# A two-layer gMLP and latent-attention trunk: the rotary score product with a 128-row stationary operand, its key zero-padded by halves

## The chip, the cores and the metric

One core of one Trainium2 chip runs the whole program in a single launch. The metric is the device time of one execution in microseconds; three runs of the kernel before gave 1175.08, 1179.63 and 1184.22 us, with a median of 1179.63 us. One more execution was recorded by the profiler, and every time of a single instruction comes from that one.

## The reference

Batch 1, 256 tokens, width 2048. A gMLP layer is followed by a layer of multi-head latent attention with 16 heads; every sub-layer is modulated by a shift, a scale and a gate worked out from a conditioning vector. What the change touches is the score of the attention: each head's key and query have a part of 128 dimensions without position and a rotary part of 64, and the rotary key is one and the same for all heads.

```python
k_rope = apply_rope(rms_norm(k_r, g_kr), cos, sin)          # (B, S, 64): one for all heads
...
s = (jnp.einsum('bqhd,bkhd->bhqk', qn_b, k_nope)            # 128 dimensions, per head
     + jnp.einsum('bqhr,bkr->bhqk', qr_b, k_rope)).astype(jnp.float32) * scale
s = jnp.where(k_pos[None, :] <= q_pos[:, None], s, -jnp.inf)
p = jax.nn.softmax(s, axis=-1).astype(v.dtype)
return jnp.einsum('bhqk,bkhd->bqhd', p, v)
```

The queries come in two blocks of 128. The rotary key of a token, k_rope, is normalised and rotated once, before the keys of the heads are made.

## The kernel before, in words

**The products over weights.** Every large product reads its weights from memory in pieces of 1 MB (`raw`, L304; four buffers, shared with the modulation's pieces `araw`, L178). ScalarE rounds a piece to `hi` (L160), VectorE subtracts to get `lo` (L162), and TensorE adds three products (hi by hi, hi by lo, lo by hi, L324) into PSUM banks. There are four pairs of `hi` and `lo` buffers, so ScalarE writes a new `hi` when TensorE is done with an old one. The output projection (`b_w_out`, 16 pieces) is the last of these products, and its results are gated, added to the residual and stored (L598, L599, L884).

**The modulation.** A step of `Ada` (L175) loads 1 MB of a modulation weight and multiplies it with the conditioning row on VectorE (L187). The last sixteen steps make the gate `ga1`; they are spread over the attention and the output projection, and TensorE turns four of their columns at a time into a piece of the gate (L229).

**The attention.** `keys(i)` and `queries(i)` make two heads at a time. A query product ends in `pq`; its heads are normalised and rotated, and TensorE turns them over (L816 for the 128 dimensions without position, L817 for the rotary ones). The two rotary parts of a pair, 64 dimensions each, are turned over together: `qrT` has the even head in rows 0 to 63 and the odd head in rows 64 to 127 (L819). `ev_dkv` makes the rotary key: it is written twice side by side into `kd`, turned over in one piece (L735), and copied to `krT` (L736), which thus holds the same 64 rows in both halves of its 128.

When both parts of a pair are there, `attend(h)` is queued for its two heads (L760) and one such entry is issued after each item of the main loop (L351). `attend(h)` issues the scores of head h and the output of the head before.

`scores(h)` has four products, two for each block of queries: L842 with the 128 dimensions without position (stationary operand 128 by 128), L843 with the 64 rotary ones (stationary operand 64 by 128, in rows 0 to 63 for an even head and 64 to 127 for an odd one, by `pb`). The first block has 128 keys, the second 256. The operands are float32, and each such product is two instructions of the same shape on TensorE, with a weight load each. VectorE then scales, masks and takes the maximum (L847), ScalarE takes the exponential (L850).

`output(h)` turns the probabilities over on TensorE (L860), copies them back (L862), multiplies with the values (L863 to L865) and gates (L868). After an odd head, four turns (L877) bring the pair's result into the form that the output projection reads.

The framework orders the instructions of each engine when the program is built, and each engine then issues its own in that order. The DMA queue of SyncE is in the order of the program text.

Of the kernel before, what the change touches and what calls it, by code (L numbers as in the profile page):

```python
# [9 lines left out]
F32 = mybir.dt.float32  # L10
# [4 lines left out]
PSUM = bass.MemoryType.PSUM  # L15

P = 128
D = 2048
S = 256
# [4 lines left out]
DR = 64  # L24
DV = 128
R = 512
EPS = 1e-6
KD = D // P
NB = 1024
# [25 lines left out]


class Banks:
    """The eight PSUM banks: some for accumulation throughout, the others shared out among streams of tiles by phase."""
    def __init__(self, tc):
        self.tc, self.phase, self.ctx = tc, -1, ExitStack()  # L60
        self.mm = self.ctx.enter_context(tc.tile_pool(name="psm", bufs=MM, space=PSUM))
# [25 lines left out]
def trunk_kernel(ctx: ExitStack, tc: tile.TileContext, a: dict, out: bass.AP):  # L87
    nc = tc.nc
    ctx.enter_context(tc.manual_schedule(engines={nc.sync.engine}))
    const = ctx.enter_context(tc.tile_pool(name="const", bufs=1))  # L90
# [5 lines left out]
    banks = Banks(tc)  # L96
# [8 lines left out]
    def bank(name, tag="aux"):  # L105
        return banks.tile(tag, name)

# [1 line left out]
    crow = slot("crow")  # L109
    nc.sync.dma_start(crow[0:1, :], a["c"])  # L110
    xt = []
# [15 lines left out]
    nhalf = const.tile([P, 4], F32, name="nhalf")  # L127
    nc.vector.memset(nhalf, -0.5)

# [1 line left out]
    def rstd_of(ms, n, scale=1.0):  # L131
        """(ms * scale + EPS) ** -0.5"""
        t = sml.tile([P, 4], F32, tag="rs0", name="rs0")
        r = sml.tile([P, 4], F32, tag="rs1", name="rs1")
        nc.vector.tensor_scalar(out=t[:, :n], in0=ms, scalar1=scale, scalar2=EPS, op0=ALU.mult, op1=ALU.add)
        nc.gpsimd.tensor_tensor(out=r[:, :n], in0=t[:, :n], in1=nhalf[:, :n], op=ALU.pow)
        return r[:, :n]
# [3 lines left out]
        nc.scalar.activation(j, src, AF.Square, scale=scale, accum_out=dst)  # L141

    def rms_rstd(pieces):
        """1/rms of the rows made of pieces."""
        n = len(pieces)
        ss = sml.tile([P, 4], F32, tag="ss4", name="ss4")
        for i, p in enumerate(pieces):
            squares(ss[:, i:i + 1], p, "a")
        return rstd_sum(ss, n, sum(p.shape[-1] for p in pieces))
# [12 lines left out]
            nc.vector.tensor_tensor(out=lo, in0=src, in1=hi.bitcast(F32), op=ALU.subtract)  # L162

    def behind(ins):
        """What follows is issued after ins, where there is one, on its engine."""
        return tc.issue_after(ins.ins) if ins else nullcontext()

    hold, queue, chain = [None], [False], []
# [43 lines left out]
            ada[background.pop(0)].step()  # L212

    class Gate:
        """A gate as rows on all partitions, by pieces of 512 columns."""
        def __init__(self, n):
            self.ada, self.rows, self.done = ada[n], None, set()

# [12 lines left out]
            return g  # L231

    class Norm:
        """x / rms(x), transposed."""
        def __init__(self, xt, name):
            self.xt = xt
            self.ts = [slot(f"{name}T{i}") for i in range(2)]
# [11 lines left out]
            nc.scalar.copy(dst, p.rearrange("p (k t) -> p k t", t=P))  # L249

        def rows(self, t):
            """The whole of token tile t, scaled as rows."""
            for q in range(4):
                self.sums(t, q)
            r = rstd_sum(self.st[t], 4, D)
            for q in range(4):
                x = self.xt[t][:, q * 512:(q + 1) * 512]
                nc.vector.tensor_scalar_mul(x, x, r)
                self.flip(t, q)
# [3 lines left out]
            self.flip(t, q)  # L263

        def finish(self, t):
            """1/rms of token tile t, broadcast over the partitions."""
            if self.rb is None:
                self.rb = const.tile([P, S], F32, name=self.name + "rb")
            r = rstd_sum(self.st[t], 4, D)
            p = bank("px")  # L270
            nc.tensor.transpose(p[:, :P], r.broadcast_to([P, P]), ident)
            return p[:, :P]
# [27 lines left out]
            return lambda c, w: self.at(w, 2 * kk + c)  # L300

    def load_split(w, kk, n, nk=2):
        """nk chunks of the contraction of w as exact pairs hi + lo; a pair of tiles holds up to NB columns in all."""
        raw = wraw.tile([P, nk, n], F32, tag="raw", name="raw")  # L304
        nc.sync.dma_start(raw, w[kk * nk * P:(kk + 1) * nk * P, :].rearrange("(c p) n -> p c n", p=P))
        per = max(1, NB // n) if n < NB else 1
        parts = []
        for c0 in range(0, nk, per):
            hi = wsp.tile([P, per, n], F32R, tag="hi", name="hi")
            lo = wsp.tile([P, per, n], F32R, tag="lo", name="lo")  # L310
            split(raw[:, c0:c0 + per, :], hi, lo)
            parts += [(hi[:, c, :], lo[:, c, :]) for c in range(per)]
        return parts

    def mms(ps, t, lh, wt, widths, first, last, apart=False):
        """Adds the chunks wt of the contraction, for token tile t, to the banks ps."""
        offs = [sum(widths[:i]) for i in range(len(widths))]
        for some in ([[i] for i in range(len(widths))] if apart else [range(len(widths))]):
            for c, (hi, lo) in enumerate(wt):
                for which, rhss in ((0, (hi, lo)), (1, (hi,))):  # L320
                    lt = lh(c, which)[:, t * P:(t + 1) * P]
                    for rhs in rhss:
                        for i in some:
                            nc.tensor.matmul(ps[i][:, :widths[i]], lhsT=lt, rhs=rhs[:, offs[i]:offs[i] + widths[i]],  # L324
                                             start=(first and c == 0 and which == 0 and rhs is hi),
                                             stop=(last and c == len(wt) - 1 and which == 1))
# [1 line left out]
    later = deque()  # L328

    def drive(items):  # L330
        """items: (prepare, compute, after). The next item is prepared before the present one is computed, or, where
        the present one ends in a chain that the next waits for, right before what follows it."""
        items = iter(items)
        nxt = next(items, None)
        ready = nxt[0]() if nxt else None
        while nxt:
            cur, got = nxt, ready
            nxt = next(items, None)
            late = len(cur) > 3
            if nxt and not late:  # L340
                queue[0] = True
                ready = nxt[0]()
                queue[0] = False
            cur[1](got)
            if nxt and late:
                queue[0] = True
                ready = nxt[0]()
                queue[0] = False
            cur[2]()
            if later:  # L350
                later.popleft()()  # L351

    class Block:
        """A product over a block of columns of w, cut along the contraction in steps of two chunks."""
        def __init__(self, lhs, w, nkk, widths, evac):
            self.lhs, self.w, self.nkk, self.widths, self.evac = lhs, w, nkk, widths, evac
            self.n = sum(widths)
# [52 lines left out]
                    bg(quota * tail if n < stop else 0.0)  # L410
                yield (prep, comp, post, "late") if then else (prep, comp, post)

# [1 line left out]
    norm0 = Norm(xt, "x")  # L414
    for t in range(NT):
        norm0.rows(t)
# [29 lines left out]
    blocks = [[in_block("v", i, None), vt[i], lambda t, n, ps, i=i: ev_v(i, t, n, ps)] for i in range(4)]  # L446
# [173 lines left out]
            b = Block(lhs_split(lambda kk: yT[kk // 4][:, (kk % 4) * 2:(kk % 4) * 2 + 2, :]), a["a_w_out"][:, i * NB:(i + 1) * NB], GW // P // 2, [512, 512], ev_o)  # L620
            yield from b.items(AQ, tail=TAIL, after=early1 if i else None, then=late1 if i else None, before=fetch, stop=STOP if i else 99)

# [1 line left out]
    at = {}  # L624

    def attention_constants():
# [26 lines left out]
        nc.vector.tensor_tensor(out=dst[:, :, 32:64], in0=dst[:, :, 32:64], in1=m[:, :, 0:32], op=ALU.add)  # L653

    rinv = const.tile([P, NT, 16], F32, name="rinv")
    krT = const.tile([P, S], F32, name="krT")
    lat, szb, yb = {}, {}, {}
    gate1 = Gate("ga1")
    w_b = a["b_w_in"]
# [22 lines left out]
        return lambda c, w: at["h"].at(w, 2 * kk + c)  # L682

    def latent(which, t, pieces, gname):
        """Normalises the row made of pieces (PSUM), and keeps it transposed as hi + lo."""
        r = rms_rstd(pieces)
        cn = scratch([P, R], "cn")
        o = 0
        for p in pieces:
            n = p.shape[-1]  # L690
            nc.scalar.activation(cn[:, o:o + n], p, AF.Identity, scale=r)
            o += n
        p = bank("px", "tr")
        for j in range(4):
            nc.tensor.transpose(p[:, j * P:(j + 1) * P], cn[:, j * P:(j + 1) * P], ident)
        if which not in lat:
            lat[which] = slot("lat" + which, F32R).rearrange("p (w k t) -> p w k t", w=2, t=S)
        lt = lat[which]
        h = scratch([P, 4, P], "hl")
        for j in range(4):  # L700
            nc.vector.tensor_scalar_mul(h[:, j, :], p[:, j * P:(j + 1) * P], col[gname][:, j:j + 1])
        split(h, lt[:, 0, :, t * P:(t + 1) * P], lt[:, 1, :, t * P:(t + 1) * P])
# [18 lines left out]
    def ev_dkv(t, n, ps):  # L721
# [3 lines left out]
        w = R - 288  # L725
# [7 lines left out]
        nc.vector.tensor_copy(kd[:, 1, :], kd[:, 0, :])  # L733
        p = bank("px", "tr")
        nc.tensor.transpose(p[:, :P], kd.rearrange("p a b -> p (a b)"), ident)  # L735
        hold[0] = nc.vector.tensor_copy(krT[:, t * P:(t + 1) * P], p[:, :P])  # L736

    def lhs_lat(which):
        return lambda c, w: lat[which][:, w, c, :]
# [86 lines left out]
    soft = {}  # L826

    def attend(h):
        """The scores of head h, and the output of the head before, whose softmax runs meanwhile."""
        if h < 16:  # L830
            scores(h)
        if h > 0:
            output(h - 1)

    def scores(h):
        i, j = divmod(h, 2)
        kT, qT, qrT = (pairs[i][n] for n in ("kT", "qT", "qrT"))
        pS = bank("pS")
        pb = j * DR
        for t, (c0, c1) in enumerate(TQ):  # L840
            nk = c1 - c0
            nc.tensor.matmul(pS[:, c0:c1], lhsT=qT[:, j, t * P:(t + 1) * P], rhs=kT[:, j, 0:nk], start=True, stop=False)  # L842
            nc.tensor.matmul(pS[:, c0:c1], lhsT=qrT[pb:pb + DR, t * P:(t + 1) * P], rhs=krT[pb:pb + DR, 0:nk], start=False, stop=True)  # L843
        pr = scratch([P, P + S], "pr", "b")
        mx = sml.tile([P, 4], F32, tag="mx", name="mx")
        for t, (c0, c1) in enumerate(TQ):
# [100 lines left out]
```

## Time and profile before

| | |
|---|---|
| runs | 1175.08, 1179.63, 1184.22 us; median 1179.63 |
| span of the profiled execution, first to last instruction | 1176.9 us; its own time outside the span is not recorded |
| mean granted TensorE clock | 0.989 |
| busy, share of the span | TensorE 95%, its weight load 78%, VectorE 82%, ScalarE 53%, GpSimd 7% |
| read from memory | 331.10 MB, 283 GB/s over the span |
| first and last score product | 973.6 and 1099.5 us after the start of the span |
| output projection's products | about 1058 to 1169 us |

A timeline row gives the start in us, the duration in us, the engine (PE is TensorE's products, PEld its weight loads, DVE VectorE, ACT ScalarE, POOL GpSimd), the line of the kernel, the operation, the tile written and those read, the shape, and how many instructions the row covers; in brackets stands the idle time before it and what ended it. Successive products overlap in the records, so what a product costs the stream is the distance from its start to the next start, not its duration. A row "128*128 128x256" is a product with 128 active rows and columns whose moving operand has 256 columns. A row of the table by windows has the window, its length, and for PE, PEld, DVE, ACT and POOL the busy time with the number of instructions, then the granted clock, the busy share of the DMA engines and their GB/s.

### The profile page before, as it was taken

Reading aid. Unit: us, or ns where it says so; the run is one execution under the profiler, and the core shown is the slowest. Engines: PE = TensorE matmul, PEld = TensorE weight load, DVE = VectorE, ACT = ScalarE, POOL = GpSimd, SP = SyncE. Lnnn points to the kernel's source line nnn. Section 1 sums busy time; section 2 is a strip of 40 time slices with the busy share of each in tenths; the row PEclk is TensorE's granted clock in tenths of the full one; section 3 lists DMA queues with packets and bytes.
Section 4 is the critical chain, followed back from the end, with each engine's and each line's share of the span. In section 5 each row is a group of like instructions: output and inputs, shape, how many; then the busy total and the mean of one; then the engine's idle time right before and its main releaser. Section 6 shows DMA issues by size and latency. Waiting matters only on the chain.

```text
span 1176.9 us, 14465 instructions
## 1 busy us (share of the span) xinstructions
PE 1113.0 (95%) x5140; PEld 915.6 (78%) x5140; DVE 963.3 (82%) x1388; ACT 624.2 (53%) x1147; POOL 78.0 (7%) x87
## 2 busy tenths in 40 slices
PE   1898999999989999999999999989999999999997
PEld 1686888888868878878878877878889788887886
DVE  1889999978988897797799889879886567677896
ACT  3663444455765434444444445457638488785332
POOL 2000000000500200000020000000000122120000
PEclk9899999999999999999999999999999999999999
DMA  5899998888788989889979998977996545254784
GB/s 221 340 350 326 337 342 335 296 310 294 252 306 301 324 302 338 336 281 346 334 263 338 326 346 316 340 275 286 354 330 199 196 141 176 89 178 182 255 303 191
DMA packets 78026, 334.14 MB, mean 284 GB/s; under 512 B 5489, under 2 KB 9969, under 8 KB 61185
## 3 DMA queue, kind: packets, MB, share of 16 engines
q1 hardware_dynamic: 76802, 331.12, 78.1%
q10 hardware_dynamic: 1152, 2.10, 0.6%
q8 instruction: 40, 0.66, 0.2%
q14 instruction: 32, 0.26, 0.1%
HBM read 331.10 MB, written 2.10 MB: 283 GB/s over the span
## 4 chain that ended last, share of the span: by engine, by line
PE 57%; DVE 17%; DMA 14%; issue 9%; ACT 3%; POOL 1%; SPq 0%; DVEq 0%; ACTq 0%; POOLq 0%
PE pm L324 45%; DMA araw<-in_ada_wT 9%; DVE lo L162 7%; DVE araw L187 4%; DMA araw<-in_kv_ada_wT 4%; PE pk L324 4%; PE pq L324 3%; PE pS L843 1%; ACT hi L160 1%; PE pS L842 1%; DVE v L463 1%; DMA raw<-in_a_w_in 1%; DVE v L543 1%; DVE sz L558 1%; ACT sq L141 1%
## 5 line engine op out<-in xcount | busy, mean ns | idle before, releaser
L160 ACT CAST hi<-raw 128x1024 fp32r<-128x1024 f32 (+2 forms) x376 | 382.6, 1031 | 408.9 <-PE pm L324 253.2
L162 DVE TENSOR_TENSOR lo<-raw,hi 128x1024 fp32r<-128x1024 f32 (+2 forms) x376 | 445.4, 1201 | 68.5 <-ACT hi L160 67.6
L187 DVE CUSTOM_DVE_ANT_0 araw<-araw,s_b,vec 128x2048 f32<-128x2048 f32 (+1 forms) x128 | 275.9, 2158 | 65.1 <-DMA araw<-in_ada_wT 46.5
L324 PE MATMUL pm<-lo,hh 128*128 128x512 f32 x768 | 252.0, 396 | 11.0 <-DVE lo L162 11.0
L324 PE MATMUL pm<-hi,hh 128*128 128x512 f32 x768 | 242.4, 394 | 5.6 <-ACT hh L286 3.4
L324 PE MATMUL pm<-hi,hl 128*128 128x512 f32 x768 | 247.3, 392 | 0.0
L324 PEld LDWEIGHTS pm<-lo,hh 128*128 128x128 f32 x768 | 143.9, 189 | 45.3 <-DVE lo L162 16.1
L324 PEld LDWEIGHTS pm<-hi,hh 128*128 128x128 f32 x768 | 145.1, 189 | 38.0 <-ACT hh L286 3.6
L324 PEld LDWEIGHTS pm<-hi,hl 128*128 128x128 f32 x768 | 144.9, 189 | 30.7 <-DVE hl L287 0.2
L324 PE MATMUL pm<-lo,shi 128*128 128x512 f32 (+1 forms) x320 | 95.3, 373 | 3.7 <-DVE lo L162 3.7
L324 PE MATMUL pm<-hi,shi 128*128 128x512 f32 (+1 forms) x320 | 94.6, 373 | 0.9 <-ACT shi L160 0.9
L324 PE MATMUL pm<-hi,slo 128*128 128x512 f32 (+1 forms) x320 | 93.9, 371 | 0.0
L324 PEld LDWEIGHTS pm<-lo,shi 128*128 128x128 f32 x320 | 58.2, 188 | 14.8 <-DVE lo L162 5.3
L324 PEld LDWEIGHTS pm<-hi,shi 128*128 128x128 f32 x320 | 58.0, 188 | 11.0 <-ACT shi L160 1.4
L324 PEld LDWEIGHTS pm<-hi,slo 128*128 128x128 f32 x320 | 58.0, 188 | 10.1
L324 PE MATMUL pm<-hi,gh 128*128 128x512 f32 x160 | 53.0, 403 | 1.1 <-ACT kn L730 1.1
L324 PE MATMUL pm<-hi,gl 128*128 128x512 f32 x160 | 53.8, 398 | 0.0
L324 PE MATMUL pm<-lo,gh 128*128 128x512 f32 x160 | 53.5, 401 | 0.0
L324 PE MATMUL pk<-hi,latkv 128*128 128x512 f32 x128 | 43.9, 411 | 0.0
L324 PE MATMUL pm<-lo,ybh 128*128 128x512 f32 x128 | 43.2, 395 | 0.0
L324 PE MATMUL pm<-hi,ybl 128*128 128x512 f32 x128 | 43.0, 395 | 0.0
L324 PE MATMUL pm<-hi,ybh 128*128 128x512 f32 x128 | 42.9, 402 | 0.0
(177 smaller groups left out, 1258.8 us busy)
## 6 DMA issues: line engine op xcount, KB each, us to landing
araw<-in_ada_wT SPq DMA_DIRECT2D x96, 1024.0 KB
raw<-in_a_w_in SPq DMA_DIRECT2D x96, 1024.0 KB
raw<-in_a_w_out SPq DMA_DIRECT2D x32, 1024.0 KB
araw<-in_kv_ada_wT SPq DMA_DIRECT2D x32, 1024.0 KB
raw<-in_b_w_in SPq DMA_DIRECT2D x16, 1024.0 KB
raw<-in_b_w_out SPq DMA_DIRECT2D x16, 1024.0 KB
raw<-in_kv_w_ukv SPq DMA_DIRECT2D x8, 1024.0 KB
raw<-in_b_w_uq SPq DMA_DIRECT2D x8, 768.0 KB
```

What stands on the lines that cost most here:

```text
L141: nc.scalar.activation(j, src, AF.Square, scale=scale, accum_out=dst)
L160: nc.scalar.copy(hi, src)
L162: nc.vector.tensor_tensor(out=lo, in0=src, in1=hi.bitcast(F32), op=ALU.subtract)
L187: nc.vector.tensor_tensor_reduce(out=t[:, c], in0=t[:, c], in1=s_b[:, c], scale=1.0, scalar=acc, op0=ALU.mult, op1=ALU.add, accum_out=dst)
L324: nc.tensor.matmul(ps[i][:, :widths[i]], lhsT=lt, rhs=rhs[:, offs[i]:offs[i] + widths[i]], start=(first and c == 0 and which == 0 and rhs ...
L463: nc.vector.tensor_tensor(out=p, in0=ps, in1=p, op=ALU.add)
L543: nc.vector.scalar_tensor_tensor(out=v, in0=v, scalar=vr[t][1], in1=gb[1], op0=ALU.mult, op1=ALU.add)
L558: nc.vector.scalar_tensor_tensor(out=y[:, sl], in0=pmix[:, sl], scalar=col["bs"][:, g:g + 1], in1=y[:, sl], op0=ALU.add, op1=ALU.mult)
L842: nc.tensor.matmul(pS[:, c0:c1], lhsT=qT[:, j, t * P:(t + 1) * P], rhs=kT[:, j, 0:nk], start=True, stop=False)
L843: nc.tensor.matmul(pS[:, c0:c1], lhsT=qrT[pb:pb + DR, t * P:(t + 1) * P], rhs=krT[pb:pb + DR, 0:nk], start=False, stop=True)
```

## The change

The stationary operand of L843 becomes the whole `qrT`, all 128 rows, both heads of the pair. The moving operand is a new, larger `krT` with two planes of 256 columns: plane 0 has the rotary key in rows 0 to 63 and zeros below, plane 1 zeros above and the key in rows 64 to 127. Head j of a pair reads plane j, so the other head's 64 rows are multiplied with zeros. GpSimd sets `krT` to zero once, and the copy at L736 is cut into two of 64 rows each. What a score is does not change.

```diff
     rinv = const.tile([P, NT, 16], F32, name="rinv")
-    krT = const.tile([P, S], F32, name="krT")
+    krT = const.tile([P, 2, S], F32, name="krT")
+    nc.gpsimd.memset(krT, 0.0)
...
         nc.tensor.transpose(p[:, :P], kd.rearrange("p a b -> p (a b)"), ident)
-        hold[0] = nc.vector.tensor_copy(krT[:, t * P:(t + 1) * P], p[:, :P])
+        nc.vector.tensor_copy(krT[0:DR, 0, t * P:(t + 1) * P], p[0:DR, :P])
+        hold[0] = nc.vector.tensor_copy(krT[DR:, 1, t * P:(t + 1) * P], p[DR:, :P])
...
         pS = bank("pS")
-        pb = j * DR
         for t, (c0, c1) in enumerate(TQ):
             nk = c1 - c0
             nc.tensor.matmul(pS[:, c0:c1], lhsT=qT[:, j, t * P:(t + 1) * P], rhs=kT[:, j, 0:nk], start=True, stop=False)
-            nc.tensor.matmul(pS[:, c0:c1], lhsT=qrT[pb:pb + DR, t * P:(t + 1) * P], rhs=krT[pb:pb + DR, 0:nk], start=False, stop=True)
+            nc.tensor.matmul(pS[:, c0:c1], lhsT=qrT[:, t * P:(t + 1) * P], rhs=krT[:, j, 0:nk], start=False, stop=True)
```

The rest of the diff takes out comments and docstrings and leaves blank lines. Lines up to 656 keep their numbers; L736 becomes lines 737 and 738, and L842 and L843 become 843 and 844.

In the built programs TensorE, ScalarE and SyncE have the same instructions in the same order before and after. Two engines get more. On VectorE, where the rotary key of the first 128 tokens is copied, the rows before are:

```order
L733 COPY kd<-kd 128x64
L135 TENSOR_SCALAR rs_7049<-ss_7047 128x1
L162 TENSOR_TENSOR lo<-raw,hi 128x1024 x3
L736 COPY krT<-px 128x128
L701 TENSOR_SCALAR hl<-px,vec 128x128 x4
```

and those of the change:

```order
L734 COPY kd<-kd 128x64
L135 TENSOR_SCALAR rs_7051<-ss_7049 128x1
L162 TENSOR_TENSOR lo<-raw,hi 128x1024 x3
L737 COPY krT<-px 64x128
L738 COPY krT<-px 64x128
L702 TENSOR_SCALAR hl<-px,vec 128x128 x4
```

One copy has become two at the same place, and the same holds for the second 128 tokens. On GpSimd, at the start of the program, the rows of the change are:

```order
masks.py:197 MEMSET ident 128x128
L657 MEMSET krT 128x512
L635 MEMSET mask 128x256
masks.py:199 ISA
masks.py:199 AFFINE_SELECT ident<-ident 128x128
L636 AFFINE_SELECT mask<-mask 128x128
```

The row of `krT` is new; the others stand as before.

## Prediction

> **What bounds the kernel now.** I read the page first, then the table by windows over the attention and the output projection, then what TensorE waited for there.
>
> ```profile
> PE 1113.0 (95%) x5140; PEld 915.6 (78%) x5140; DVE 963.3 (82%) x1388; ACT 624.2 (53%) x1147; POOL 78.0 (7%) x87
> ...
> PE 57%; DVE 17%; DMA 14%; issue 9%; ACT 3%; POOL 1%; SPq 0%; DVEq 0%; ACTq 0%; POOLq 0%
> ```
>
> ```profile
> 970.00:1000.00 30.00, 30.00 (x161) 24.66 (x159) 22.54 (x76) 26.35 (x104) 8.16 (x10) 1.00 0.55 184
> ...
> 1080.00:1125.00 45.00, 45.00 (x227) 36.10 (x226) 38.66 (x95) 17.13 (x31) 0.00 (x0) 1.00 0.73 257
> 1125.00:1169.00 44.00, 44.00 (x198) 36.31 (x197) 36.56 (x66) 15.22 (x16) 0.00 (x0) 1.00 0.73 261
> ```
>
> ```profile
> PE px L784 <- ACT kt L783: 0.5, 1, 0.5
> ```
>
> TensorE is the busiest engine of the span, and from 970 to 1169 us, where the changed products lie, it never stops. The last row is all that TensorE waited for there: one wait of 0.5 us. So time taken out of TensorE's stream counts unless a neighbour becomes the bound. But "busy" hides what the stream loses between products, so I looked at one head instruction by instruction: its products, then its weight loads.
>
> ```profile
> 1016.10 0.38 PE L842 MATMUL pS<-pair 128*128 128x128 f32 x2
> 1016.41 0.48 PE L843 MATMUL pS<-krT,pair 64*128 64x128 f32 x2
> 1016.83 0.70 PE L842 MATMUL pS<-pair 128*128 128x256 f32 x2
> 1017.46 0.70 PE L843 MATMUL pS<-krT,pair 64*128 64x256 f32 x2
> 1018.09 0.44 PE L877 MATMUL px<-ident,szb 128*128 128x128 f32 x2
> 1018.36 0.49 PE L860 MATMUL pT<-ident,pr 128*128 128x128 f32 x3
> ```
>
> ```profile
> 1015.93 0.36 PEld L842 LDWEIGHTS pS<-pair 128*128 128x128 f32 x2
> 1016.41 0.29 PEld L843 LDWEIGHTS pS<-krT,pair 64*128 64x128 f32 x2
> ```
>
> From start to start the five pairs take 0.31, 0.42, 0.63, 0.63 and 0.27 us, together 2.26. Pairs of the same size with no 64-row product next to them go faster:
>
> ```profile
> 1100.88 0.38 PE L863 MATMUL pT<-pair,pts 128*128 128x128 f32 x2
> 1101.10 0.39 PE L864 MATMUL pT<-pair,pts 128*128 128x128 f32 x2
> ```
>
> ```profile
> 1006.18 0.38 PE L842 MATMUL pS<-pair 128*128 128x256 f32 x1
> 1006.39 0.27 PE L784 MATMUL px<-ident,kt 128*128 128x128 f32 x1
> ```
>
> A pair with 128 columns takes 0.22 us (1100.88 to 1101.10), a single product with 256 columns 0.21, so a pair about 0.43. The load rows show why the head is slower. The load of the full-size L842 starts at 1015.93, before its product and under the one ahead. The load of L843 starts at 1016.41, together with its own product, though the stream of L842 should have ended at 1016.10 + 0.22 = 1016.32. So at a change from 128 to 64 rows the stream stands for 0.09 us and then waits for a load that lies open, about 0.11 (0.42 for the L843 pair less 0.22 for streaming and 0.09 for the stand after it). The change back costs the same: the second L842 pair takes 0.63 instead of 0.43.
>
> **The change part by part.** *The products.* With all 128 rows there is no change of shape, and a head should take three pairs of 0.22 and two of 0.43, 1.52 us: 2.26 - 1.52 = 0.74 saved. Four weight loads a head make the count:
>
> ```profile
> L842 PEld LDWEIGHTS pS<-pair x64: 186/189/192, 973.4 to 1098.7; 128*128 128x128 f32 x64
> L843 PEld LDWEIGHTS pS<-krT,pair x64: 182/184/186, 973.9 to 1099.3; 64*128 64x128 f32 x64
> ```
>
> 64 loads are 16 heads: 16 x 0.74 = 11.84 us. In six of the heads a weight product follows instead of a turn; there the open load costs more:
>
> ```profile
> 1099.85 0.72 PE L324 MATMUL pm<-hi,ybh 128*128 128x512 f32 x2
> 1100.41 0.63 PE L324 MATMUL pm<-lo,ybh 128*128 128x512 f32 x2
> ```
>
> That pair takes 0.56 against 0.47 for the next (1100.41 to 1100.88), 0.09 lost, where the turn above lost 0.27 - 0.22 = 0.05. Six times the difference is some 0.25, and the whole is 12.1 us. The zeros cost nothing to stream: the pairs at 1016.83 and 1017.46 have 128 and 64 rows and the same 0.63. The wider load takes 189 instead of 184 ns, at most 0.3 us over all 64, under a running product.
>
> *What is added.* GpSimd's memset of 512 columns stands between these:
>
> ```profile
> 0.93 0.32 POOL L635 MEMSET mask<- 128x256 f32 x1
> ...
> 11.74 2.30 POOL L124 PARTITION_BROADCAST s_b<-crow  x1 [9.64 <-ACT sq L141]
> ```
>
> At twice the 256 columns it takes up to 0.64 us, at least the 0.32 of the row; GpSimd then idles 9.64 us before anything that others need, so it costs nothing; uncovered it would be 0.64. The two copies of 64 rows replace one of 128:
>
> ```profile
> 926.31 0.28 DVE L736 COPY krT<-px 128x128 f32<-128x128 f32 x1
> ...
> 930.58 1.23 DVE L162 TENSOR_TENSOR lo<-raw,hi 128x1024 fp32r<-128x1024 f32 x1 [1.16 <-ACT hi L160]
> ```
>
> A copy of half the rows takes between 0.14 and 0.28 us, so the two add 0 to 0.28 for each block of tokens. The 1.16 us of idle VectorE hides it, and the scores read it only at 973.9; uncovered, twice 0.28. No DMA and no queue order changes, and TensorE's new wait on the memset was met 900 us before.
>
> *What comes back.* The one place where TensorE already waits is this piece of the chain:
>
> ```profile
> 994.97 1.57 PE pq L324 x9
> ...
> 996.63 0.57 ACT sq L141 x4
> ...
> 1000.75 0.38 ACT kt L783
> 1001.13 0.04 issue
> 1001.18 0.59 PE px L784 x2
> ```
>
> From 996.63 to 1001.13 ScalarE and VectorE work through the normalising of a pair without a stop, set off by a product that ends at 996.54. Four heads' scores come before 1001.18, but only three before 996.54, so the fourth head's 0.74 turns into a longer wait. ScalarE is busy 26.35 of 30 us there, so it may not follow the first three fully; this can cost between 0 and 3 x 0.74 = 2.2. The later pairs have the same chain with more room, and TensorE waited in none of them; I take 0.5 for all of this, near the lower end since those waits are absent. The sum is 12.1 - 0.74 - 0.5 = 10.9 us. Against the span that is 1176.9 - 10.9 = 1166.0. The median of the runs is 2.7 us above that span, and 1179.63 - 10.9 = **1168.7 us**.
>
> *The output projection* must follow, too. The end of its supply:
>
> ```profile
> 1125.89 1.06 ACT L160 CAST hi<-raw 128x1024 fp32r<-128x1024 f32 x1 [3.96 <-PE pm L324]
> ...
> 1156.05 2.01 ACT L160 CAST hi<-raw 128x1024 fp32r<-128x1024 f32 x2 [4.51 <-DMA raw<-in_b_w_out]
> ```
>
> ```profile
> 1162.47 2.36 DVE L162 TENSOR_TENSOR lo<-raw,hi 128x1024 fp32r<-128x1024 f32 x2
> ```
>
> ```profile
> 1166.09 0.39 PE L324 MATMUL pm<-lo,ybh 128*128 128x512 f32 x1
> ```
>
> At 1156.05 ScalarE waits for a load, not for TensorE: the last pieces arrive at memory's pace. The first `lo` of the last two is done at 1162.47 + 1.2 = 1163.7 and used at 1166.09, a margin of 2.4 us. The loads are issued as buffers come free, though, and at 1125.89 it is still TensorE that frees them. So this tail should move earlier as a whole.
>
> **The rivals.** *Memory sets the end.* If the tail does not move, only its 2.4 us are won: 1177.2. For it speaks the row at 1156.05, against it the one at 1125.89. *ScalarE and VectorE take half.* If each of the eight pairs loses one head's 0.74 as the first does, 5.9 us go back: 12.1 - 5.9 = 6.2, that is 1173.4. For it speaks 26.35 of 30; against it that in the later windows ScalarE is far less busy (17.13 of 45). *The loads stay open.* Only the stands go, four a head of 0.09, 16 x 0.36 = 5.8 us, less the 0.74: 1174.6. [...] The load at 1015.93, 128 rows high and ahead of its product, goes against it here. *The stand has nothing to do with the 64 rows*, but with adding to the same bank; then nothing changes, 1179.6. Against it: the second instruction of each L842 pair adds to the same bank without a stand. *Slower:* TensorE outruns the loads in the tail, waits, and its clock falls.
>
> ```profile
> 948.50:952.00 3.50, 3.50 (x10) 2.73 (x9) 2.34 (x6) 1.93 (x4) 0.00 (x0) 0.51 0.37 139
> 941.10:948.10 7.00, 5.15 (x27) 4.02 (x26) 5.20 (x13) 5.69 (x18) 2.94 (x4) 1.00 0.56 163
> ```
>
> After TensorE stood 1.85 of 7 us, the clock was 0.51 for 3.5 us, some 1.75 lost. With the win down to 2.4 us the second such window makes the kernel slower; three give 1179.63 - 2.4 + 5.3 = 1182.5. Against it: from 970 to 1169 the clock is 1.00, and the tail has no such wait.
>
> **How the numbers follow.** The forecast gets 0.70, memory's end 0.08, half lost 0.10, open loads 0.03, no effect 0.06, slower 0.03. About 1% is what a measurement of this kernel can tell from no change, and faster by over 1% means below 1167.8. The forecast lies 0.9 us above that, with runs that scatter by 4.5 us to either side, and the full 12.1 us would give 1167.5: nearly half of the forecast's 0.70 falls below, 0.33, and some 0.02 of the rest. Slower by over 1% needs several windows of a low clock or a scatter that no row shows, 0.03 with the slower case; the remaining 0.62 is within 1%. The range goes down to the full win less the runs' scatter, 1167.5 - 4.5 = 1163, and up to memory's end, 1177.5; the forecast's own is 1165 to 1172.
>
> **What would show it.** Right: in a head of the changed kernel the five pairs stand 0.22, 0.22, 0.43, 0.43 and 0.22 us apart, the loads of the rotary products start under the product ahead, and from 1002 us on everything is earlier by a growing amount, some 11 us at the output projection. Step by step wrong: pairs of 0.31 and 0.42 again (the stand is of another kind); pairs of 0.33 with loads that start with their products (open loads); a sum of waits of TensorE between 970 and 1169 of several us, on ScalarE's `kt` (neighbours) or on `lo` after 1125 (memory); a clock under 1.00 in that stretch (slower).

## The result

| | before | changed |
|---|---|---|
| median of 5 runs | 1179.63 us (1175.08 to 1184.22) | 1167.49 us (1163.16 to 1169.84) |
| ratio, with its 95% interval | 1 | 0.989 [0.9853, 0.9927] |
| span of the profiled execution | 1176.9 us | 1161.4 us |
| first score product | 973.6 us | 969.3 us |
| from the first score product to the end | 203.3 us | 192.2 us |

The kernel is faster by about 1%, as forecast; the forecast was 1168.7. The span fell by 15.5 us, more than the change can give, but 4.4 us of it were there before the first score product. What the change is worth is the last row: 11.1 us. In the table of runs below, one execution each of `e_group` and `e_pair2` lies over 1.5% above the fastest of its kernel and counts as slow, so the median includes it and the ratio does not.

TensorE's busy time on the page fell by 11.1 us as well, from 1113.0 us. That the two numbers agree is chance, since over the first 968 us, ahead of the scores, TensorE's busy time scatters by several us between executions of one kernel: 910.7 and 908.0 us before (`e_before`), 915.8 and 909.7 us with the change (`e_after`). The page of the changed kernel:

```profile
PE 1101.9 (95%) x5140; PEld 917.8 (79%) x5140; DVE 962.6 (83%) x1390; ACT 623.6 (54%) x1147; POOL 77.2 (7%) x88
```

The head of which the prediction showed the products and the weight loads, in the changed kernel (L843 and L844 are the former L842 and L843):

```profile
1008.68 0.38 PE L843 MATMUL pS<-pair 128*128 128x128 f32 x2
1008.90 0.39 PE L844 MATMUL pS<-krT,pair 128*128 128x128 f32 x2
1009.12 0.60 PE L843 MATMUL pS<-pair 128*128 128x256 f32 x2
1009.56 0.59 PE L844 MATMUL pS<-krT,pair 128*128 128x256 f32 x2
1009.99 0.38 PE L878 MATMUL px<-ident,szb 128*128 128x128 f32 x2
1010.21 0.49 PE L861 MATMUL pT<-ident,pr 128*128 128x128 f32 x3
```

```profile
1008.51 0.36 PEld L843 LDWEIGHTS pS<-pair 128*128 128x128 f32 x2
1008.79 0.30 PEld L844 LDWEIGHTS pS<-krT,pair 128*128 128x128 f32 x2
```

The starts are 0.22, 0.22, 0.44, 0.43 and 0.22 us apart, together 1.53 us instead of 2.26. The load of the rotary product now starts at 1008.79, 0.11 before its product at 1008.90, under the product ahead. What TensorE waited for from 960 us to the end of its products, and the chain that leads to that wait:

```profile
PE px L786 <- ACT kt L785: 1.2, 1, 1.2
```

```profile
987.73 2.12 PE pq L324 x12
...
989.93 0.57 ACT sq L141 x4
...
994.06 0.38 ACT kt L785
994.43 0.05 issue
994.48 0.59 PE px L786 x2
```

It is the same single wait as before, 1.2 us instead of 0.5. The supply of the output projection moved along with TensorE:

```profile
1110.40 1.06 ACT L160 CAST hi<-raw 128x1024 fp32r<-128x1024 f32 x1 [3.96 <-PE pm L324]
...
1140.95 2.00 ACT L160 CAST hi<-raw 128x1024 fp32r<-128x1024 f32 x2 [4.54 <-DMA raw<-in_b_w_out]
```

```profile
1147.36 2.36 DVE L162 TENSOR_TENSOR lo<-raw,hi 128x1024 fp32r<-128x1024 f32 x2
```

```profile
1150.60 0.39 PE L324 MATMUL pm<-lo,ybh 128*128 128x512 f32 x1
```

The cast at 1125.89 us now starts at 1110.40 and the one at 1156.05 at 1140.95. That is 15.5 and 15.1 us earlier, of which 4.4 lie ahead of the scores, so the tail moved by some 11 us with TensorE. The first `lo` of the last two is done 1150.60 - (1147.36 + 1.2) = 2.0 us before TensorE uses it, where it was 2.4.

### The profile page after: what moved, and what is told of

It reads as the page before. It is cut to its first block, busy times and chain, and to the rows that moved or that the text cites. A ratio compares the mean times of both kernels' runs of the same rounds, so it can differ in the third digit from the quotient of the medians.

```text
span 1161.4 us, 14469 instructions
## 1 busy us (share of the span) xinstructions
PE 1101.9 (95%) x5140; PEld 917.8 (79%) x5140; DVE 962.6 (83%) x1390; ACT 623.6 (54%) x1147; POOL 77.2 (7%) x88
## 4 chain that ended last, share of the span: by engine, by line
PE 75%; DVE 10%; DMA 7%; issue 5%; ACT 2%; POOL 1%; SPq 0%; DVEq 0%; ACTq 0%; POOLq 0%
PE pm L324 62%; PE pk L324 4%; DVE lo L162 3%; DMA araw<-in_ada_wT 3%; DVE araw L187 3%; PE pq L324 3%; DMA araw<-in_kv_ada_wT 3%; PE pmix L554 1%; DVE v L463 1%; PE pS L843 1%; PE pS L844 1%; ACT hi L160 1%; DMA raw<-in_a_w_out 1%; DMA x<-in_x 1%; PE px L247 1%
```

## The experiments

Each timed kernel is compared with runs of the kernel before on the same chip. Besides the time I read from each profile the stretch from the first score product to the end, since it turned out to repeat to 0.1 us (203.3 in three profiles, 192.2 in two):

| run | median, us | ratio, interval | first score product, us | span, us | stretch, us |
|---|---|---|---|---|---|
| before | 1179.63 | | 973.6 | 1176.9 | 203.3 |
| e_before | 1184.01 (one run) | | 979.0 | 1182.3 | 203.3 |
| e_added | 1182.48 (one run) | | 977.4 | 1180.7 | 203.3 |
| changed | 1167.49 | 0.989 [0.9853, 0.9927] | 969.3 | 1161.4 | 192.2 |
| e_after | 1170.15 | 0.9933 [0.9907, 0.996] | 979.1 | 1171.3 | 192.2 |
| e_group | 1173.24 | 0.9955 [0.9932, 0.9977] | 972.5 | 1170.5 | 198.1 |
| e_alt6 | 1187.09 | 1.0083 [1.0054, 1.0112] | 978.2 | 1189.6 | 211.4 |
| e_alt6_full | 1171.65 | 0.9955 [0.993, 0.9979] | 977.4 | 1175.0 | 197.7 |
| e_pair | 1176.0 | 0.9972 [0.9947, 0.9997] | 974.5 | 1174.8 | 200.3 |
| e_pair_full | 1171.85 | 0.9953 [0.9926, 0.9981] | 974.3 | 1171.1 | 196.8 |
| e_pair2 | 1180.41 | 1.0017 [0.9981, 1.0052] | 968.1 | 1169.7 | 201.5 |

**Before and after once more.** The first is the kernel before without an edit, the second the changed one.

> The kernel before once more, for the scatter between executions. In the profiles shown, the first score product starts at 973.6 us before and at 969.1 after, though nothing ahead of it can have changed in cost. If that 4.5 us is scatter of the part before the attention, this run's first score product starts somewhere from 967 to 978 us, and the stretch from the first score product to the end is that of before, 203 us, to within 1 us. If the change itself made the early part faster, this run starts its scores at 973 to 974 again.

> The changed kernel once more. Theory (all scatter lies ahead of the attention, and what the change is worth is fixed): its first score product starts somewhere from 967 to 980 us, the stretch from there to the end is 192.2 us as in the first profile, to within 0.2 us, 11.1 us less than the 203.3 of three profiles with 64-row products, and the times come out 11 us under those of the kernel before. Rival (the stretch itself scatters, and the first profile was a lucky one): the stretch differs by more than 1 us.

The first scores start at 979.0 and 979.1 us, and the stretches are 203.3 and 192.2 again. So the 4.4 us ahead of the scores in the first pair of profiles were scatter; over all eleven profiles the first score product starts between 968.1 and 979.1. The times of `e_after` were expected to fall by 11 us and fell by 7.4, or 0.67%. A gain of 11.1 of 1178 us would be a ratio of 0.9906: the first interval, [0.9853, 0.9927], holds it, and the second, [0.9907, 0.996], begins just above it. Taken alone, the times of `e_after` point to a slightly smaller gain; why they do is not shown.

**The added parts alone.**

```diff
+    krT = const.tile([P, 2, S], F32, name="krT")
+    nc.gpsimd.memset(krT, 0.0)
...
-rhs=krT[pb:pb + DR, 0:nk]
+rhs=krT[pb:pb + DR, j, 0:nk]
```

(and the two copies, as in the change.)

> Only what the change adds: the larger rotary key, its zeroing and the two copies; the score products stay 64 rows high. Theory (the gain is the products' shape alone): the five pairs of a head take 0.31, 0.42, 0.63, 0.63 and 0.27 us as before, and the stretch from the first score product to the end stays 203 us, to within 1 us. Rival (the layout of the key or the time of the copies has a share): the stretch gets shorter or longer by some us.

The stretch is 203.3 us and the head has its old gaps, so the layout of the key is worth nothing either way and the whole gain of the stretch is the shape of the products. The zeroing and the copies stand ahead of the first score product, where the stretch cannot see them; the first score product at 977.4 us lies within the scatter of that part, and what the two cost is read from their neighbours further down.

**Two changes of shape instead of four.**

```diff
-nc.tensor.matmul(pS[:, c0:c1], lhsT=qT[:, j, t * P:(t + 1) * P], rhs=kT[:, j, 0:nk], start=True, stop=False)
-nc.tensor.matmul(pS[:, c0:c1], lhsT=qrT[pb:pb + DR, t * P:(t + 1) * P], rhs=krT[pb:pb + DR, 0:nk], start=False, stop=True)
...
+one, two = (nope, rot) if t == 0 else (rot, nope)
+nc.tensor.matmul(pS[:, c0:c1], start=True, stop=False, **one)
+nc.tensor.matmul(pS[:, c0:c1], start=False, stop=True, **two)
```

`nope` holds the operands of L842, `rot` those of L843.

> The kernel before with the second block's two products exchanged, so that the order in a head is 128, 64, 64, 128 rows: two changes of shape instead of four, with the same loads and columns. Theory (a change of shape costs a stand of 0.09 us and an open load of 0.11, and 64-row products next to each other cost neither): the pairs take 0.31, 0.33, 0.52, 0.54 and 0.22 us, 1.92 together instead of 2.26, 16 x 0.34 = 5.4 us less, some 1174. Rival (every 64-row product pays its own open load): the third pair takes 0.63, 2.03 together, 3.7 us less. Rival (the stand has to do with adding to the same columns, not with the shape): 2.26 again, no gain.

One head of it:

```profile
1013.70 0.38 PE L845 MATMUL pS<-pair 128*128 128x128 f32 x2
1014.01 0.48 PE L846 MATMUL pS<-krT,pair 64*128 64x128 f32 x2
1014.34 0.59 PE L845 MATMUL pS<-krT,pair 64*128 64x256 f32 x2
1014.86 0.70 PE L846 MATMUL pS<-pair 128*128 128x256 f32 x2
1015.40 0.38 PE L880 MATMUL px<-ident,szb 128*128 128x128 f32 x2
1015.62 0.49 PE L863 MATMUL pT<-ident,pr 128*128 128x128 f32 x3
```

0.31, 0.33, 0.52, 0.54 and 0.22 us, 1.92 together, to the hundredth what the theory gave. The second rotary product, a 64-row one behind a 64-row one, pays neither a stand nor an open load at its start (it starts 0.33 us after the first, which is 0.22 for the first's streaming and 0.11 for the first's own open load); it only has the stand behind it, where the next change of shape is (0.52 us, 0.43 and 0.09). The rivals' 2.03 and 2.26 are out. The stretch is 5.2 us shorter than before (5.4 expected), the time lower by 0.45%. TensorE's one wait is 0.8 us instead of 0.5.

**Six changes of shape, and the same cut with 128 rows.**

```diff
-        for t, (c0, c1) in enumerate(TQ):
+        for t, c0, c1, k0 in ((0, 0, P, 0), (1, P, 2 * P, 0), (1, 2 * P, 3 * P, P)):
...
-rhs=kT[:, j, 0:nk]
+rhs=kT[:, j, k0:k0 + P]
-rhs=krT[pb:pb + DR, 0:nk]
+rhs=krT[pb:pb + DR, k0:k0 + P]
```

(With 128 rows, the last line reads `krT[:, j, k0:k0 + P]` and the rest is the changed kernel.)

> The kernel before with the second block's 256 keys cut in two, so that a head has six pairs of 128 columns that alternate between 128 and 64 rows: six changes of shape instead of four, the same columns. Theory: 0.31, five times 0.42 and 0.27 us, 2.68 together instead of 2.26, 16 x 0.42 = 6.7 us more, some 1186. Rival (the cost goes with the columns of the 64-row products, not with the number of changes): 2.26 again, 1179 to 1180.

> The changed kernel with the same cut of the 256 keys in two: six pairs of 128 columns that alternate between the two operands as in the run with six changes, but all 128 rows high. Theory (it is the shape): seven pairs of 0.22 us in a row, 1.54 together against 1.52, so the time of the changed kernel, some 1168. Rival (alternating operands, more loads or more groups cost something by themselves): pairs of 0.3 us and more, and a time between 1170 and 1175.

The first of the two has this head:

```profile
1022.60 0.39 PE L841 MATMUL pS<-pair 128*128 128x128 f32 x2
1022.91 0.49 PE L842 MATMUL pS<-krT,pair 64*128 64x128 f32 x2
1023.33 0.49 PE L841 MATMUL pS<-pair 128*128 128x128 f32 x2
1023.75 0.48 PE L842 MATMUL pS<-krT,pair 64*128 64x128 f32 x2
...
1025.00 0.55 PE L859 MATMUL pT<-ident,pr 128*128 128x128 f32 x3
```

and the second these rows:

```profile
1017.14 0.39 PE L842 MATMUL pS<-pair 128*128 128x128 f32 x2
1017.36 0.39 PE L843 MATMUL pS<-krT,pair 128*128 128x128 f32 x2
1017.59 0.39 PE L842 MATMUL pS<-pair 128*128 128x128 f32 x2
...
1018.48 0.49 PE L860 MATMUL pT<-ident,pr 128*128 128x128 f32 x3
```

With alternating shapes a pair of 128 columns takes 0.31 and then 0.42 us, with one shape 0.22 each. The operands alternate in both, so it is the shape and not the alternation, the number of loads or the adding to the same bank. The time of the first came out as expected (some 1186 us; 1187.09 measured), with 8.1 us more in the stretch; TensorE's waits on ScalarE and VectorE grew from 0.5 to 2.1 us, which leaves 6.5 for the stream. That of the second did not: its stream is as fast as the changed kernel's, but the stretch is 5.5 us longer. With more products the framework ordered TensorE's instructions anew, and TensorE's waits grew from 1.2 to 5.9 us:

```profile
PE pm L324 <- ACT ybh L160: 2.3, 2, 1.2
PE px L786 <- ACT kt L785: 1.2, 1, 1.2
PE pT L863 <- DVE pts L862: 0.8, 1, 0.8
PE px L877 <- DVE szb L868: 0.8, 1, 0.8
PE pm L324 <- DVE ybl L162: 0.8, 1, 0.8
```

These 4.7 us are most of the 5.5; the rest was not taken apart. The measured time, 1171.65, lies where the rival put it (1170 to 1175) and would have spoken for the wrong theory; the rows decide. Apart from the shapes, TensorE's order is the same in `e_alt6` and `e_alt6_full`, so the fairest measure of six changes is one against the other: 211.4 - 197.7 = 13.7 us, although the second waits 3.8 us longer.

**Both heads of a pair together.** The 64-row products of an even and an odd head read different halves of the 128 rows, and in this order they stand next to each other:

```diff
+if j == 0:
+    both[:] = [bank("pS") for _ in range(2)]
+    for t, (c0, c1) in enumerate(TQ):
...
+        for f in ((nope, rot) if t == 0 else (rot, nope)):
+            for w in range(2):
+                f(w)
+pS = both[j]
```

Here `nope(w)` and `rot(w)` issue the two products of head w of the pair. `e_pair2` also makes each product follow the one ahead on TensorE and takes both softmaxes at once; `e_pair_full` has the order of `e_pair` with 128-row products.

> The kernel before (64 rows) with both heads of a pair scored together, the rotary products of the two heads next to each other, one in the upper half of the rows and one in the lower, into two PSUM banks: two changes of shape for two heads. Theory A (products in different halves still go one after the other): the rotary products of a pair take 2 x 0.22 + 2 x 0.43 us and two heads take 3.2 us together against 2.8 in the changed kernel, so slower than it by some 3 us, about 1171. [...]

> The changed kernel (128 rows) with both heads of a pair scored together in the same order as the run before: what the order itself costs. If the order costs nothing, the time is that of the changed kernel, some 1168, with pairs of 0.22 and 0.43 us throughout; if holding a second bank of scores delays the softmax or what follows it, TensorE waits more than the 1.2 us that it waits in the attention of the changed kernel.

> 64-row products again, with both heads of a pair scored together as before, but now the rotary products of the two heads always stand next to each other, and both heads' softmax follows at once. In the first run of this kind, where the two stood together they started 7 ns apart, and two heads took 2.36 us from the first score product to the next turn against 2.62 in the changed kernel. Theory A (the stream decides): 8 x 0.26 = 2.1 us less than the changed kernel, a stretch from the first score product to the end of 190 us. Theory B (the order of the softmax decides): TensorE waits more than the 1.2 us of the changed kernel, by 3 to 5 us as in the two runs with pairs, and the stretch is 193 to 195 us, longer than the 192.2 of the changed kernel.

Two heads of `e_pair` where the rotary products stand together:

```profile
1026.15 0.61 PE L842 MATMUL pS<-pair 128*128 128x128 f32 x4
1026.69 0.93 PE L845 MATMUL pS<-krT,pair 64*128 64x128 f32 x8
1027.54 1.13 PE L842 MATMUL pS<-pair 128*128 128x256 f32 x4
1028.51 0.49 PE L866 MATMUL pT<-ident,pr 128*128 128x128 f32 x3
```

The eight rotary instructions of the two heads go through in 0.85 us (1026.69 to 1027.54) with both changes of shape in it; one after the other they would need 2 x 0.22 + 2 x 0.43 and 0.2 for the changes, 1.5. In the records the two halves start 7 ns apart; the rows from 1026.65 to 1026.75 us have both:

```profile
1026.48 0.28 PE L842 MATMUL pS<-pair 128*128 128x128 f32 x1
1026.69 0.38 PE L845 MATMUL pS<-krT,pair 64*128 64x128 f32 x2
```

So theory A, by which they go one after the other, is out: here the products of the two halves run at the same time. Two heads take 2.36 us to the next turn where the changed kernel needs 2.62.

But the stretches are 200.3 us (there the framework separated the halves in half of the pairs), 196.8 with 128 rows in the same order, and 201.5 with the halves always together: longer than 192.2 in all three. The expectations missed this: theory A put `e_pair` only some 3 us behind the changed kernel, and the two theories for `e_pair2` gave 190 and 193 to 195. `e_pair_full` differs from the changed kernel in the order alone, so scoring two heads at once costs 196.8 - 192.2 = 4.6 us. `e_pair` has the order of `e_pair_full` on TensorE and is 3.5 us longer still: the heads that the framework separated still have changes of shape, and what the others gain by the overlap does not make up for it. TensorE waits in the three runs for 3.6, 4.3 and 8.8 us instead of 1.2, so of what they are longer than the changed kernel (8.1, 4.6 and 9.3 us), 2.4, 3.1 and 7.6 are longer waits; the rest was not taken apart. That the waits come from a softmax that is bunched is the likely reading, not shown by a run of its own. In `e_pair2` 6.7 of the 8.8 us end on VectorE, most of them on its copies of the probabilities and its gating:

```profile
PE pT L872 <- DVE pts L871: 3.3, 3, 1.9
PE px L886 <- DVE szb L877: 2.0, 3, 1.2
PE pT L869 <- DVE ybl L162: 1.4, 1, 1.4
```

No version of this kind beat the changed kernel. An order that has both the overlap and the old spacing of the softmax was not tried.

## Why the prediction was right

**The price of a change of shape** held in size: 2.26 - 1.53 = 0.73 us a head were gained where 0.74 were forecast, and the count of changes moves the stretch as it should, from none (192.2) over two (198.1) and four (203.3) to six (211.4, with 1.6 of it in longer waits). That it is the shape was argued from one gap in the load rows; the runs with two and six changes and the one with six alternations and no change show it. Of the price of some 0.2 us, the stand is 0.09 and the open load behind it, the larger half, 0.11; both are the author's estimate from the starts of one head, and `e_group` met the five gaps worked out from them. What TensorE does during the stand is not shown.

**The rival with open loads** is out: the load at 1008.79, 128 rows high, runs under a 128-row product and starts 0.11 us before its own, and the rotary pair takes 0.22 us, not 0.33. Its time, 1174.6, was not met.

**What is added** cost nothing that a row shows. The memset took 0.53 us (forecast 0.32 to 0.64), and GpSimd later idles for 10.34 us. The two copies took 0.28 and 0.29 us, each as long as the one of 128 rows, so my lower bound, half for half the rows, was wrong by its idea. VectorE waits 0.30 us for ScalarE soon after the first two, and 0.73 us after the second two:

```profile
0.93 0.53 POOL L657 MEMSET krT<- 128x512 f32 x1
...
12.90 2.30 POOL L124 PARTITION_BROADCAST s_b<-crow  x1 [10.34 <-issue]
```

```profile
921.83 0.28 DVE L737 COPY krT<-px 64x128 f32<-64x128 f32 x1
922.12 0.29 DVE L738 COPY krT<-px 64x128 f32<-64x128 f32 x1
...
925.64 1.23 DVE L162 TENSOR_TENSOR lo<-raw,hi 128x1024 fp32r<-128x1024 f32 x1 [0.30 <-ACT hi L160]
```

**What comes back** was 0.7 us at the place named, the `kt` wait that grew from 0.5 to 1.2, against 0.74. For the later pairs 0.5 were set aside; 12.1 - 0.7 - 11.1 leaves 0.3, which was not taken apart. The forecast of 10.9 was 0.2 too low.

**The rivals.** Memory did not set the end: the tail moved by some 11 us as a whole, and its margin only went from 2.4 to 2.0 us. ScalarE took one head's saving once, not eight times. The stall was not of another kind (`e_alt6_full`). The clock stayed up where the slower rival needed it to fall:

```profile
969.00:1153.00 184.00, 182.76 (x1000) 159.21 (x999) 153.10 (x412) 112.46 (x356) 20.42 (x22) 1.00 0.60 209
```

**What was luck** is how near the median came. It fell by 12.1 us where the stretch fell by 11.1, and in `e_after` the same kernel is only 7.4 us below the one before. Scatter of the part ahead of the scores is the likely reason for both, but most of the executions behind the medians were not profiled. The prediction gave 0.62 to a change within 1%, and the two ratios, 0.989 and 0.9933, lie on either side of that line. What tests the mechanism is the stretch, 11.1 us against 10.9.

## What to carry to other kernels

In this kernel a product with fewer rows than its neighbours was not cheap: it streamed no faster (0.63 us for the pair of 64 rows and the pair of 128 with 256 columns before), and each change of shape, into it and out of it, cost about 0.2 us of TensorE's time (0.73 us for the four of a head; by the estimate above, the stream stands for 0.09 and then waits 0.11 for a weight load that nothing covers). Zero rows in one operand cost nothing in the stream (0.22 and 0.43 us a pair, as for full operands). Where they can't be had, small products next to each other save half of the changes (5.2 us here); in different halves of the rows they even ran at once (starts 7 ns apart in `e_pair`), but no order with that beat the zero rows here. Where most of the scatter lies ahead of the part that was changed, compare the stretch from that part's first instruction to the end: here it repeats to 0.1 us in five profiles while the runs scatter by 4 to either side.

## What the runs showed of the hardware that was not expected

The part ahead of the scores, the same in all kernels but for the zeroing and the copies, takes between 968 and 979 us. One place is visible in `e_before`:

```profile
274.65 0.80 PE L324 MATMUL pm<-hi,hh 128*128 128x512 f32 x1 [4.33 <-DVE v L471]
275.24 0.63 PE L324 MATMUL pm<-lo,hh 128*128 128x512 f32 x1
275.67 0.63 PE L324 MATMUL pm<-hi,hl 128*128 128x512 f32 x1
```

```profile
274.70:280.30 5.60, 5.60 (x13) 4.41 (x14) 3.95 (x5) 2.60 (x8) 0.00 (x0) 0.50 0.69 208
```

TensorE waited 4.33 us there, against 0.5 in the first profile of the same kernel, and then had a granted clock of 0.50 for 5.6 us, with 0.43 us from product to product (0.23 at 271.00 us in the first profile, at a clock of 1.00). Together that is 3.8 + 2.8 = 6.6 us, and the first score product came 5.4 us later than in that profile. Other profiles go with it: where this wait is 3.2 us (`e_after`), 4.0 (`e_added`) and 4.3 (`e_before`), the scores start at 979.1, 977.4 and 979.0; where it is 0.3 (changed), 0.5 (before) or absent (`e_group`), at 969.3, 973.6 and 972.5. Why the wait is long in some executions was not looked into.
